# Order edges, four moved block differences and a rotation of three PSUM banks in a one-core decoder block

## The chip, the core and the metric

One core of a Trainium2 chip runs the whole program. The metric is device time in microseconds; of several executions the median is taken. The engines are TensorE (PE, with its weight loads as PEld), VectorE (DVE), ScalarE (ACT), GpSimd (POOL) and SyncE (SP), which issues the weight loads.

## The reference

A decoder block for 256 tokens of width 2048, in float32, one layer:

```python
h = h + hybrid_mixer(rmsnorm(h), ...)      # projection, GLA + short conv, gated merge, w_out
h = h + swiglu(rmsnorm(h), w_gate_up, w_down)
return rmsnorm(h, final_norm_w)

# hybrid_mixer
q, k, v, g_out, gk_low, gate_b, gate_c, xc, merge_a, merge_b = split(h @ w_in)
log_g = log_sigmoid(gk_low @ w_gk_up + b_gk_up) / 16
o = gla_chunked(q, k, v, log_g)            # 4 heads, chunks of 64: exp of cumulative decays
y_a = rmsnorm(o, gla_norm_w) * silu(g_out)
y_b = gate_b * causal_depthwise_conv(gate_c * xc, conv_w)     # 3 taps
merged = sigmoid(merge_a) * y_a + sigmoid(merge_b) * y_b
return merged @ w_out
```

The feed-forward width is 5632; the weights come to some 330 MB.

## The kernel before

**Products.** Every product is exact to nearly float32: each weight piece (128 x 1024 values, 512 KB) is loaded by SP, copied on ScalarE into a rounded high part (`high`, L217) and subtracted on VectorE to give a low part (`low`, L222); `mm3` (L326 to L328) does three matmuls for each product. A piece makes 12 full-width matmuls (128x512), or 24 of half that width. The code counts pieces in *ticks*; pieces are loaded five ticks ahead (`LOOK`), and `later`, `at` and `one_at_a_time` hang side work on ticks: a function runs, and so issues its instructions, at its tick.

**Stages.** First the GLA: for each of four heads `k`, `q` (columns) and `v` (tokens). Beside it the decay tables are built: `tables_within` (L673) makes `eq` and `ek` on VectorE and exponentiates `ek` (L678), L705 does `eq` at tick 23, `tables_across` (L682) makes `exk` and `exq` with five GpSimd instructions (L686 to L690) and exponentiates them (L691, L692). `decayed` (L722) multiplies a head's keys and queries by its part of the four tables (L726). `scores` (L730) multiplies them on PE into a score bank `sc_ps`, copies it out under a mask (L742) and without (L743), and splits it (L745, L747); `attend` (L754) is nine matmuls into two banks `o_ps` that alternate with the score banks. `x_blocks` (L711) prepares sums and differences of quarters of the normalized input, four blocks, at ticks 42, 47, 52 and 57: they are input to the next stage.

Then the gates: pairs of column groups (`gc` with `xc`, and so on) are done with seven block products in place of eight (`sevens`, 28 small pieces, five banks of `b0` to `b4`), and between these pieces stand the pieces of *plain groups* (`eights`, L354): `g`, `ma`, `gb`, `mb`. A plain group accumulates two banks (one for each half of the tokens) over eight pieces; then `gate`'s `done` empties them with a sigmoid or silu on ScalarE and a product on VectorE (`gated`, L840 to L844). `conv` (L806) shifts the pair's product by DMA and does five VectorE instructions (L827) at ticks 12 to 16 after; `merge` (L829) combines (L832, L833), and `transpose_block` (L541, bank `trb`) turns the merged half on PE.

Then `w_out` in four groups (`wo0` to `wo3`), each followed by `transpose_gain` (L524: two transpose groups `tr`, a scaled copy, high and low parts, and sums of blocks), then the feed-forward part in three rounds of `sevens` with plain groups, and down-projections `dn`, which take two of `b0` to `b5` in turn.

**PSUM.** Eight banks. `bank` without a tag deals `b0` to `b5` in turn (`k`, `q`, `v`, `wo`, `dn`); `aux` alternates `ax0` and `ax1` (scores, attention, `tr`); plain groups always take `b5` and `ax1`; `transpose_block` always takes `ax0`. A tile in a bank waits until the tile before it in that bank has been read.

**Order.** No order is written out for the engines. A planner goes through the instructions with its own durations; on each engine it issues, of those that it takes to be ready, the one that the code issued first. An instruction that it takes to be ready early can so pass others of its engine. On the chip every engine then works strictly in the planned order, and waits at each instruction for what it needs.

Of the kernel before, what the change touches and what calls it, by code (L numbers as in the profile page):

```python
# [8 lines left out]
F32 = mybir.dt.float32  # L9
F32R = mybir.dt.float32r  # L10
I8 = mybir.dt.int8
AF = mybir.ActivationFunctionType
ALU = mybir.AluOpType
AX = mybir.AxisListType

P = 128
T = 256
NT = T // P
# [147 lines left out]
@with_exitstack  # L166
def block_kernel(ctx, tc, x, xt, cols_in, gkw_in, gku_in, gnw, conv_w, finw, w_in, w_out, w_gu, w_dn, out):
    nc = tc.nc
    mats = {"w_in": w_in, "w_out": w_out, "w_gu": w_gu, "w_dn": w_dn}

    const = ctx.enter_context(tc.tile_pool(name="const", bufs=1))
# [8 lines left out]
    def bank(shape, name, tag=None):  # L180

        if tag is None:
            tag = f"b{turn['b'] % 6}"
            turn["b"] += 1
        return psum.tile(shape, F32, tag=tag, name=name)

    def aux(shape, name):

        turn["ax"] += 1
        return bank(shape, name, f"ax{turn['ax'] % 2}")  # L190

# [97 lines left out]
    def later(delay, fn):  # L292

        pending.append((count["tick"] + delay, fn))
# [35 lines left out]
    def tok_piece(ps, t, piece, k0, first, last, a):  # L330
        hi, lo, n = piece
        for k in range(n):
            ah, al = a(t, k0 + k)
            mm3(ps, ah, al, hi[:, k, :], lo[:, k, :], first and k == 0, last and k == n - 1)
# [16 lines left out]

        return lambda t, k: (hi[k // 4][:, k % 4, t * P:(t + 1) * P], lo[k // 4][:, k % 4, t * P:(t + 1) * P])

    def eights(key, a, done, tags=("b5", "ax1")):  # L354

        ps = [bank([P, 512], f"{key}_{t}", tag) for t, tag in enumerate(tags)]
        for k0 in range(0, KC, 2):
            piece, _ = yield
            for t in range(NT):
                tok_piece(ps[t], t, piece, k0, k0 == 0, k0 == KC - 2, a)  # L360
        done(ps)

    def quad(ps, pair, piece, first, last, onto=False):

# [119 lines left out]
    xh = aT.tile([P, KC, T], F32R, tag="ah", name="xh")  # L484
    xl = aT.tile([P, KC, T], F32R, tag="al", name="xl")
# [38 lines left out]
    def transpose_gain(q, hi, lo, tiles):  # L524

        raw = dpool.tile([P, 4, T], F32, tag="sg7", name="hraw")
        for m in range(2):
            ps = aux([P, 2, T], "tr")
            for j in range(2):
                for t in range(NT):  # L530
                    c = 4 * q + 2 * m + j
                    nc.tensor.transpose(out=ps[:, j, t * P:(t + 1) * P], in_=h[:, t, c * P:(c + 1) * P], identity=ident)
            for j in range(2):
                c = 4 * q + 2 * m + j
                nc.scalar.activation(raw[:, 2 * m + j, :], ps[:, j, :], AF.Copy, scale=ffc[:, c:c + 1])
        cs = slice(4 * q, 4 * q + 4)
        nc.scalar.copy(hi[:, cs, :], raw)
        nc.vector.tensor_tensor(out=lo[:, cs, :], in0=raw, in1=hi[:, cs, :].bitcast(F32), op=ALU.subtract)
        sum_blocks(raw, q, tiles, dpool.tile([P, 4, 2, P], F32, tag="sg8", name="hsum"))

    def transpose_block(src, t, hi, lo):  # L541

        ps = bank([P, 4, P], "trb", "ax0")
        for j in range(4):
            nc.tensor.transpose(out=ps[:, j, :], in_=src[:, j * P:(j + 1) * P], identity=ident)
        ts = slice(t * P, (t + 1) * P)
        nc.scalar.copy(hi[:, :, ts], ps)
        nc.vector.tensor_tensor(out=lo[:, :, ts], in0=ps, in1=hi[:, :, ts].bitcast(F32), op=ALU.subtract)
# [73 lines left out]
    for j in range(4):  # L622
        later(H_AT[j], lambda j=j: load_x(j))
        later(SQ_AT[j], lambda j=j: x_squares(j))
# [27 lines left out]
    eq = gpool.tile([P, NM, T], F32, tag="eq", name="eq")  # L652
    ek = gpool.tile([P, NM, T], F32, tag="ek", name="ek")

    inv = 1.0 / 16.0
# [12 lines left out]
    def sum_decay(m0):  # L668
        for m in range(m0, m0 + 4):
            nc.vector.tensor_tensor_scan(out=bc[:, m, :], data0=restart, data1=zm[:, m, :],  # L670
                                         initial=0.0, op0=ALU.mult, op1=ALU.add)

    def tables_within():  # L673

        for n in (0, 2):
            nc.vector.tensor_tensor(out=eq[:, :, n * C:(n + 1) * C], in0=ch(n), in1=last(n), op=ALU.subtract)
            nc.vector.tensor_copy(eq[:, :, (n + 1) * C:(n + 2) * C], ch(n + 1))
        nc.scalar.activation(ek, eq, AF.Exp, scale=-inv)  # L678

    across = {}  # L680

    def tables_across():  # L682

        exk = across["k"] = gpool.tile([P, NM, P], F32, tag="exk", name="exk")
        exq = across["q"] = gpool.tile([P, NM, P], F32, tag="exq", name="exq")
        nc.gpsimd.tensor_tensor(out=exk[:, :, 0:C], in0=last(0), in1=ch(0), op=ALU.subtract)  # L686
        nc.gpsimd.tensor_tensor(out=exk[:, :, 0:C], in0=exk[:, :, 0:C], in1=last(1), op=ALU.add)
        nc.gpsimd.tensor_tensor(out=exk[:, :, C:P], in0=last(1), in1=ch(1), op=ALU.subtract)
        nc.gpsimd.tensor_copy(exq[:, :, 0:C], ch(2))
        nc.gpsimd.tensor_tensor(out=exq[:, :, C:P], in0=ch(3), in1=last(2), op=ALU.add)  # L690
        nc.scalar.activation(exk, exk, AF.Exp, scale=inv)  # L691
        nc.scalar.activation(exq, exq, AF.Exp, scale=inv)  # L692

    def at(tick, fn):
        later(tick - count["tick"], fn)
# [6 lines left out]
    at(20, lambda: sum_decay(0))  # L702
    at(21, lambda: sum_decay(4))
    at(22, tables_within)
    at(23, lambda: nc.scalar.activation(eq, eq, AF.Exp, scale=inv))  # L705
    at(25, tables_across)


    xsums = (sT.tile([P, 4, 4, 2, P], F32R, tag="sh", name="sh"), sT.tile([P, 4, 4, 2, P], F32R, tag="sl", name="sl"))

    def x_blocks(q):  # L711
        pair = gpool.tile([P, NM, T], F32, tag="bc", name="xraw")
        raw, work = pair[:, 0:4, :], pair[:, 4:8, :].rearrange("p s (j c) -> p s j c", c=P)
        cs = slice(4 * q, 4 * q + 4)
        nc.vector.tensor_tensor(out=raw, in0=xh[:, cs, :].bitcast(F32), in1=xl[:, cs, :].bitcast(F32), op=ALU.add)
        sum_blocks(raw, q, xsums, work)

    for q in range(4):
        at(42 + 5 * q, lambda q=q: x_blocks(q))


    def decayed(i, kr, qr):  # L722
# [27 lines left out]
    o = [omain.tile([P, NT, DV], F32, tag=f"m{i}", name="o") for i in range(H)]  # L750
# [19 lines left out]
    for i in range(H):  # L770
# [20 lines left out]
        for t in range(NT):  # L791
            nc.scalar.activation(vh[:, t, :], vps[t], AF.Copy, scale=r1[:, t:t + 1])
            nc.vector.scalar_tensor_tensor(out=vl[:, t, :], in0=vps[t], scalar=r1[:, t:t + 1],
                                           in1=vh[:, t, :].bitcast(F32), op0=ALU.mult, op1=ALU.subtract)
# [9 lines left out]
    us, ya, sb, merge_at = {}, {}, {}, {}  # L804

    def conv(i):  # L806
        u = us[i]
        u1 = ew.tile([P, NT, 512], F32, tag="u1", name="u1")
        u2 = ew.tile([P, NT, 512], F32, tag="u2", name="u2")
        taps = ew.tile([P, 3, 512], F32, tag="taps", name="taps")  # L810
        nc.gpsimd.dma_start(taps, conv_w[:, :, i * 512:(i + 1) * 512].to_broadcast([P, 3, 512]))
        nc.gpsimd.memset(u1[0:1, 0, :], 0.0)
        nc.gpsimd.memset(u2[0:2, 0, :], 0.0)
        nc.gpsimd.dma_start(u1[1:113, :, :], u[0:112, :, :])
        nc.gpsimd.dma_start(u2[2:114, :, :], u[0:112, :, :])
        nc.gpsimd.dma_start(u1[113:128, :, :], u[112:127, :, :])
        nc.gpsimd.dma_start(u2[114:128, :, :], u[112:126, :, :])
        nc.gpsimd.dma_start(u1[0:1, 1, :], u[127:128, 0, :])
        nc.gpsimd.dma_start(u2[0:2, 1, :], u[126:128, 0, :])

        def taps_of(j):
            return taps[:, j:j + 1, :].to_broadcast([P, NT, 512])

        for n, (dst, src, by, op) in enumerate(((u1, u1, 1, ALU.mult), (u2, u2, 0, ALU.mult), (u, u, 2, ALU.mult),
                                                (u1, u1, u2, ALU.add), (u, u, u1, ALU.add))):
            by = taps_of(by) if isinstance(by, int) else by
            later(CONV_AT + n, lambda d=dst, s=src, y=by, o=op: nc.vector.tensor_tensor(out=d, in0=s, in1=y, op=o))  # L827

    def merge(i, ts):  # L829

        v = sb[i][:, ts, :]
        nc.vector.tensor_tensor(out=v, in0=v, in1=us[i][:, ts, :], op=ALU.mult)  # L832
        later(1, lambda: nc.vector.tensor_tensor(out=v, in0=v, in1=ya[i][:, ts, :], op=ALU.add))  # L833
        if mh[i] is None:
            mh[i] = omain.tile([P, 4, T], F32R, tag=f"m{i}", name="mh")
            ml[i] = oside.tile([P, 4, T], F32R, tag=f"m{i}", name="ml")
        for t in range(ts.start, ts.stop):
            one_at_a_time(3, lambda t=t: transpose_block(sb[i][:, t, :], t, mh[i], ml[i]))
# [29 lines left out]
    def gate_pair(pair):  # L868
# [8 lines left out]
        def done(t, one, two):  # L877
            if pair[0][:-1] == "gc":
                nc.vector.scalar_tensor_tensor(out=two, in0=one, scalar=r1sq[:, t:t + 1], in1=two,
                                               op0=ALU.mult, op1=ALU.mult)  # L880
                if t == 0:
                    later(1, lambda: conv(i))
                    merge_at[i] = count["tick"] + CONV_AT + 7
            else:
# [30 lines left out]
    for n in range(4):  # L915
        cs = slice(n * 512, (n + 1) * 512)
# [91 lines left out]
    for part, (f0, f1) in enumerate(PARTS):  # L1008
# [16 lines left out]
        for e in down:  # L1025
            key, k0 = e
            n = int(key.split("_")[1])
            c0, w = DOWN[part][n]
            cs = slice(c0, c0 + w)
# [24 lines left out]


CONV_AT = 12
H_AT = (2, 4, 6, 8)
SQ_AT = (5, 7, 9, 11)
WARM = 9
# [54 lines left out]
```

## Time and profile before

| | us |
|---|---|
| median of 3 runs (lowest, highest) | 1533.85 (1528.16, 1534.53) |
| the profiled execution, its own time | 1535.26 |
| its span, first to last instruction | 1533.6 |
| PE busy, share of the span | 1510.4, 98% |
| DVE busy | 1173.5, 77% |
| ACT busy | 832.1, 54% |
| POOL busy | 36.6, 2% |
| mean granted clock of TensorE | 0.996 |

Busy time of PE is that of pipelined matmuls: each overlaps the next, so the distance between two starts tells more than a duration. A note such as `[2.89 <-ACT sch L745]` behind an instruction says that its engine was idle for 2.89 us before it and what ended the idle time.

### The profile page before, as it was taken

The page shows a single profiled execution, that of the slowest core. Times are in us where ns is not written, and L with a number is a line of the kernel's source. Part 1 is how long each engine was busy: PE and PEld are TensorE (multiplying, and loading weights), DVE is VectorE, ACT ScalarE, POOL GpSimd, SP SyncE. Part 2 cuts the span into 40 slices and gives each one's busy share as a digit, 9 for nine tenths or more (in the row PEclk, how much of TensorE's full clock was granted, in tenths as well). Part 3 has the DMA queues.
Part 4 walks back from the last instruction along what each step waited for, and adds up shares of the span by engine and source line. Part 5 has one row for each costly group of instructions (what it writes and reads, how often), then busy time and mean ns, then how long its engine had stood idle before and what let it go on. Part 6 is the DMA issues. An engine that isn't in the chain of part 4 may idle for free.

```text
span 1533.6 us, 19370 instructions
## 1 busy us (share of the span) xinstructions
PE 1510.4 (98%) x7153; PEld 1262.0 (82%) x7153; DVE 1173.5 (77%) x1173; ACT 832.1 (54%) x936; POOL 36.6 (2%) x61
## 2 busy tenths in 40 slices
PE   9989999999999999999999999999999999999998
PEld 8979988888787788878788888888888888888887
DVE  5787557979879879965668899855889975678764
ACT  6755445555654555654556555633555653455543
POOL 0020000000000000000000000000000000000000
PEclk9999999999999999999999999999999999999999
DMA  9645557878776888786765767866677886566872
GB/s 321 222 150 158 172 158 248 276 228 259 260 246 212 286 261 257 242 263 206 224 178 178 263 221 250 312 200 178 219 248 224 273 272 192 178 229 197 249 222 92
DMA packets 96399, 346.00 MB, mean 226 GB/s; under 512 B 11092, under 2 KB 11220, under 8 KB 96176
## 3 DMA queue, kind: packets, MB, share of 16 engines
q1 hardware_dynamic: 92928, 333.77, 68.0%
q0 software_dynamic: 2944, 9.41, 2.5%
q10 hardware_dynamic: 432, 1.57, 0.3%
q8 instruction: 56, 0.92, 0.2%
q14 instruction: 39, 0.32, 0.1%
HBM read 338.45 MB, written 2.10 MB: 222 GB/s over the span
## 4 chain that ended last, share of the span: by engine, by line
PE 92%; DVE 3%; issue 1%; ACT 1%; DMA 1%; POOL 1%; SPq 0%; DVEq 0%; ACTq 0%
PE fg L326 7%; PE fg L328 7%; PE fg L327 7%; PE dn L326 5%; PE dn L327 5%; PE dn L328 5%; PE gc L326 3%; PE fu L326 3%; PE fu L328 3%; PE fu L327 3%; PE gc L328 3%; PE gc L327 3%; PE gb L326 2%; PE wo L326 2%; PE mb L326 2%; PE gb L327 2%
## 5 line engine op out<-in xcount | busy, mean ns | idle before, releaser
L222 DVE TENSOR_TENSOR lo<-raw,hi 128x1024 fp32r<-128x1024 f32 (+1 forms) x517 | 628.1, 1219 | 231.3 <-PE dn L326 74.8
L217 ACT CAST hi<-raw 128x1024 fp32r<-128x1024 f32 (+1 forms) x517 | 539.9, 1050 | 409.1 <-PE dn L328 114.1
L217 ACT CAST hi<-x 128x1024 fp32r<-128x1024 f32 x108 | 113.7, 1053 | 185.6 <-DVE x L244 130.0
L222 DVE TENSOR_TENSOR lo<-x,hi 128x1024 fp32r<-128x1024 f32 x108 | 132.1, 1223 | 31.8 <-ACT hi L217 18.7
L326 PE MATMUL dn<-lo,acth 128*128 128x512 f32 (+1 forms) x376 | 141.7, 377 | 0.0
L328 PE MATMUL dn<-hi,acth 128*128 128x512 f32 (+1 forms) x376 | 141.3, 376 | 0.0
L327 PE MATMUL dn<-hi,actl 128*128 128x512 f32 (+1 forms) x376 | 141.2, 376 | 0.0
L326 PE MATMUL fg<-lo,hh 128*128 128x512 f32 x312 | 121.6, 390 | 0.0
L328 PE MATMUL fg<-hi,hh 128*128 128x512 f32 x312 | 121.5, 389 | 0.0
L327 PE MATMUL fg<-hi,hl 128*128 128x512 f32 x312 | 121.4, 389 | 0.0
L244 DVE TENSOR_TENSOR x<-x,raw 128x1024 f32<-128x1024 f32 x72 | 87.9, 1220 | 7.2 <-DMA raw<-in_w_in_dram 3.5
L328 PEld LDWEIGHTS dn<-hi,acth 128*128 128x128 f32 x376 | 70.8, 188 | 13.0
L326 PEld LDWEIGHTS dn<-lo,acth 128*128 128x128 f32 x376 | 70.8, 188 | 12.7
L327 PEld LDWEIGHTS dn<-hi,actl 128*128 128x128 f32 x376 | 70.8, 188 | 12.6
L328 PE MATMUL fu<-hi,hh 128*128 128x512 f32 x192 | 74.7, 389 | 0.0
L326 PE MATMUL fu<-lo,hh 128*128 128x512 f32 x192 | 74.7, 389 | 0.0
L327 PE MATMUL fu<-hi,hl 128*128 128x512 f32 x192 | 74.7, 389 | 0.0
L326 PEld LDWEIGHTS fg<-lo,hh 128*128 128x128 f32 x312 | 58.6, 188 | 12.5 <-DVE h L1044 0.3
L328 PEld LDWEIGHTS fg<-hi,hh 128*128 128x128 f32 x312 | 58.6, 188 | 12.4
L327 PEld LDWEIGHTS fg<-hi,hl 128*128 128x128 f32 x312 | 58.6, 188 | 12.1
L326 PE MATMUL fg<-lo,sh 128*128 128x512 f32 x160 | 63.8, 399 | 0.0
L328 PE MATMUL fg<-hi,sh 128*128 128x512 f32 x160 | 62.5, 391 | 0.0
(245 smaller groups left out, 3067.8 us busy)
## 6 DMA issues: line engine op xcount, KB each, us to landing
raw<-in_w_in_dram SPq DMA_DIRECT2D x255, 512.0 KB, 4.6
raw<-in_w_gu_dram SPq DMA_DIRECT2D x176, 512.0 KB, 4.4
raw<-in_w_dn_dram SPq DMA_DIRECT2D x88, 512.0 KB, 4.3
raw<-in_w_out_dram SPq DMA_DIRECT2D x32, 512.0 KB, 4.2
x<-in_w_gu_dram SPq DMA_DIRECT2D x20, 512.0 KB, 5.4
y<-in_w_gu_dram SPq DMA_DIRECT2D x20, 512.0 KB, 3.9
y<-in_w_in_dram SPq DMA_DIRECT2D x16, 512.0 KB, 4.2
x<-in_w_in_dram SPq DMA_DIRECT2D x16, 512.0 KB, 4.9
```

Of the source, the lines that this page charges most:

```text
L217: nc.scalar.copy(hi[:, ks, :], raw[:, ks, :])
L222: nc.vector.tensor_tensor(out=lo[:, ks, :], in0=raw[:, ks, :], in1=hi[:, ks, :].bitcast(F32), op=ALU.subtract)
L244: nc.vector.tensor_tensor(out=x, in0=x, in1=other, op=ALU.add)
L326: nc.tensor.matmul(ps, lhsT=sh, rhs=ml, start=first, stop=False, skip_group_check=onto)
L327: nc.tensor.matmul(ps, lhsT=sl, rhs=mh, start=False, stop=False, skip_group_check=onto)
L328: nc.tensor.matmul(ps, lhsT=sh, rhs=mh, start=False, stop=last, skip_group_check=onto)
```

## The change

Five edits. (1) A planner edge puts the exponentials of `exk` and `exq` behind that of `eq` on ScalarE (`issue_after`: order of issue, no wait for its end). (2) The first instruction of each of the four `x_blocks` is kept behind whatever VectorE instruction the code issued just before it (`pin`), and the blocks go to ticks 50, 54, 58 and 62. (3) The convolution's five and (4) the merge's two VectorE instructions are kept in the same way. (5) Plain groups take two of three banks, `b5`, `ax0` and `ax1`, in turn; both kinds of transposes take, each time, the oldest one that no open group holds. `g0` keeps `b3` and `b4`.

```diff
+    pin = tc.keep_in_program_order
...
+    lent = ["b5", "ax0", "ax1"]
...
-    def eights(key, a, done, tags=("b5", "ax1")):
-
-        ps = [bank([P, 512], f"{key}_{t}", tag) for t, tag in enumerate(tags)]
+    def eights(key, a, done, tags=None):
+
+        mine = tags or [lent.pop(0) for _ in range(NT)]
+        ps = [bank([P, 512], f"{key}_{t}", tag) for t, tag in enumerate(mine)]
...
         done(ps)
+        if tags is None:
+            lent.extend(mine)
...
-            ps = aux([P, 2, T], "tr")
+            lent.append(lent.pop(0))
+            ps = bank([P, 2, T], "tr", lent[-1])
...
-        ps = bank([P, 4, P], "trb", "ax0")
+        lent.append(lent.pop(0))
+        ps = bank([P, 4, P], "trb", lent[-1])
...
+    first_exp = []
...
-        nc.scalar.activation(ek, eq, AF.Exp, scale=-inv)
+        first_exp.append(nc.scalar.activation(ek, eq, AF.Exp, scale=-inv).ins)
...
-        nc.scalar.activation(exk, exk, AF.Exp, scale=inv)
-        nc.scalar.activation(exq, exq, AF.Exp, scale=inv)
+        with tc.issue_after(first_exp[-1]):
+            nc.scalar.activation(exk, exk, AF.Exp, scale=inv)
+            nc.scalar.activation(exq, exq, AF.Exp, scale=inv)
...
-    at(23, lambda: nc.scalar.activation(eq, eq, AF.Exp, scale=inv))
+    at(23, lambda: first_exp.append(nc.scalar.activation(eq, eq, AF.Exp, scale=inv).ins))
...
-        nc.vector.tensor_tensor(out=raw, in0=xh[:, cs, :].bitcast(F32), in1=xl[:, cs, :].bitcast(F32), op=ALU.add)
+        pin(nc.vector.tensor_tensor(out=raw, in0=xh[:, cs, :].bitcast(F32), in1=xl[:, cs, :].bitcast(F32), op=ALU.add))
...
-        at(42 + 5 * q, lambda q=q: x_blocks(q))
+        at(X_AT[q], lambda q=q: x_blocks(q))
...
-            later(CONV_AT + n, lambda d=dst, s=src, y=by, o=op: nc.vector.tensor_tensor(out=d, in0=s, in1=y, op=o))
+            later(CONV_AT + n, lambda d=dst, s=src, y=by, o=op: pin(nc.vector.tensor_tensor(out=d, in0=s, in1=y, op=o)))
...
-        nc.vector.tensor_tensor(out=v, in0=v, in1=us[i][:, ts, :], op=ALU.mult)
-        later(1, lambda: nc.vector.tensor_tensor(out=v, in0=v, in1=ya[i][:, ts, :], op=ALU.add))
+        pin(nc.vector.tensor_tensor(out=v, in0=v, in1=us[i][:, ts, :], op=ALU.mult))
+        later(1, lambda: pin(nc.vector.tensor_tensor(out=v, in0=v, in1=ya[i][:, ts, :], op=ALU.add)))
...
+X_AT = (50, 54, 58, 62)
```

## Rows read from the trace of the kernel before

**Rows 1.** The page, first part: busy us, share of the span, instructions.

```profile
PE 1510.4 (98%) x7153; PEld 1262.0 (82%) x7153; DVE 1173.5 (77%) x1173; ACT 832.1 (54%) x936; POOL 36.6 (2%) x61
```

**Rows 2.** Stretches: length, busy us (instructions) by engine, granted clock, DMA share, GB/s.

```profile
100.00:120.00 20.00, 15.08 (x69) 11.99 (x69) 19.24 (x31) 13.27 (x21) 0.62 (x2) 0.83 0.49 149
120.00:240.00 120.00, 120.00 (x712) 107.18 (x711) 69.40 (x81) 52.87 (x69) 2.19 (x4) 1.00 0.59 177
480.00:540.00 60.00, 56.53 (x248) 45.06 (x247) 52.46 (x50) 32.91 (x37) 0.52 (x1) 1.00 0.75 258
800.00:820.00 20.00, 20.00 (x94) 16.66 (x93) 14.25 (x16) 12.26 (x18) 0.00 (x0) 1.00 0.53 159
820.00:840.00 20.00, 20.00 (x94) 16.36 (x93) 19.92 (x24) 15.29 (x22) 0.00 (x0) 1.00 0.62 179
```

**Rows 3.** Timeline of TensorE, scores and attention: start, length, instruction [idle before, releaser].

```profile
95.53 1.05 PE L737 MATMUL sc_ps<-eq,ek 128*128 128x128 f32 x8
...
101.40 0.39 PE L328 MATMUL v<-hi,xh 128*128 128x512 f32 x1
...
103.44 0.39 PE L328 MATMUL v<-hi,xh 128*128 128x512 f32 x1
106.72 0.49 PE L326 MATMUL o_ps<-vl,sch 128*128 128x512 f32 x1 [2.89 <-ACT sch L745]
...
109.98 0.80 PE L326 MATMUL o_ps<-vl,sch 128*128 128x512 f32 x1 [1.78 <-ACT scr L743]
...
115.95 0.40 PE L328 MATMUL v<-hi,xh 128*128 128x512 f32 x1
```

**Rows 4.** Timeline of ScalarE, exponentials of the tables.

```profile
85.65 1.06 ACT L691 ACTIVATE exk<-exk 128x1024 f32<-128x1024 f32 x1 [7.20 <-POOL exk L687]
...
88.20 1.90 ACT L678 ACTIVATE ek<-eq 128x2048 f32<-128x2048 f32 x1
```

**Rows 5.** Timeline of GpSimd, the tables across chunks.

```profile
77.53 6.08 POOL L686 TENSOR_TENSOR exk<-bc 128x512 f32<-128x512 f32 x1 [26.90 <-DVE bc L670]
...
86.15 1.05 POOL L690 TENSOR_TENSOR exq<-bc 128x512 f32<-128x512 f32 x1
```

**Rows 6.** Timeline of VectorE, tables to scores.

```profile
80.01 0.42 DVE L677 COPY eq<-bc 128x512 f32<-128x512 f32 x1
...
82.62 0.75 DVE L777 TENSOR_TENSOR kr<-k,rb 128x256 f32<-128x256 f32 x2
90.13 0.69 DVE L726 TENSOR_TENSOR ek<-ek,kr 128x512 f32<-128x512 f32 x1 [6.76 <-ACT ek L678]
...
94.96 0.42 DVE L726 TENSOR_TENSOR exk<-exk,kr 128x256 f32<-128x256 f32 x1
...
98.31 1.22 DVE L715 TENSOR_TENSOR xraw<-xh,xl 128x1024 f32<-128x1024 f32 x1
...
105.40 0.43 DVE L742 COPY_PREDICATED scr<-mask,sc_ps 128x256 f32<-128x256 int8 x1
```

**Rows 7.** Waits of TensorE, 235 to 760: us in total, times, longest.

```profile
PE gb L326 <- DVE ya L844: 3.0, 3, 1.5
PE g L326 <- DVE sb L844: 1.4, 1, 1.4
...
PE ma L326 <- ACT ya L853: 1.0, 1, 1.0
...
PE gc L326 <- DVE lo L222: 0.5, 2, 0.3
```

**Rows 8.** Timeline of TensorE, from the last `ma` group to `gb`.

```profile
683.88 0.39 PE L328 MATMUL ma<-hi,xh 128*128 128x512 f32 x1
685.78 0.50 PE L326 MATMUL gb<-lo,xh 128*128 128x512 f32 x1 [1.52 <-DVE ya L844]
```

**Rows 9.** Timeline of VectorE, the second merge's sum.

```profile
492.32 1.22 DVE L833 TENSOR_TENSOR sb<-sb,ya 128x1024 f32<-128x1024 f32 x1
```

**Rows 10.** Waits of VectorE, 340 to 760: us in total, times, longest.

```profile
DVE u L827 <- DMA u<-u: 7.8, 2, 4.4
```

## Prediction

> **What bounds the kernel now.** I read the page's first part, then the stretch table, then TensorE's own timeline and its waits. PE is busy for 1510.4 of 1533.6 us [rows 1], so only its 23 us of idle time, and any time at the low clock, can be won. Some 10 us of that lie at the very start and end, which the change does not touch. Of the rest the largest piece is one stretch: between 100 and 120 us PE is busy for 15.08 of 20 us and its granted clock averages 0.83; from 120 to 240 us it never pauses [rows 2]. The other losses are single waits between 240 and 760 us [rows 7].
>
> The timeline of the bad stretch [rows 3] is to be read by distances between starts. A full-width matmul normally starts 0.227 us after the one before it (9 steps from 101.40 to 103.44). From the `v` matmul at 103.44 to the one at 115.95 there are 18 such steps, which should take 4.09 us and took 12.51: **8.42 us lost**. Two waits make most of it: 2.89 us for the head's split scores, 1.78 us for the copy of the next head's. The 14 steps from 109.98 to 115.95 then average 0.43 us, the 1.2 GHz level; the granted clock fell after these two pauses.
>
> Why are the scores late? ScalarE had nothing to do for 7.20 us because `exk`'s exponential was at the head of its queue and GpSimd had not finished that table; `ek`'s exponential, whose input VectorE had completed by 80.43, ran behind it at 88.20 [rows 4 to 6]. VectorE in turn waited 6.76 us for `ek` [rows 6]. Then, from 98.31, `x_blocks` took VectorE: the masked copy of scores that were computed at 95.53 to 96.8 [rows 3] ran only at 105.40 [rows 6]. I counted the order of VectorE's instructions against the order in which the code issues them: the first of the four `x_blocks` runs 35 places early, the fourth 45. Nothing needs their result before the first gate group with products of sums, at about 240 us.
>
> **The change part by part.**
>
> *Exponentials.* With `exk` and `exq` queued behind `eq`, ScalarE can run `ek` at about 80.5 (1.90 us), one weight cast (the size of `exk`, 1.06) and `eq` (the size of `ek`), to about 85.4; `exk`'s input is there at 85.6 and `exq`'s at 87.2 [rows 4, 5]. The last of the first head's four products, at 94.96 before [rows 6], could then come near 89. PE reaches its score matmuls at 95.53 in any case, so this alone removes little; it frees VectorE and ScalarE of the pile of casts and low parts that they worked off between 90 and 106.
>
> *x_blocks.* One block is two instructions of 1.22 us and four of 0.42 on VectorE (lengths of [rows 6]) with a cast on ScalarE: 4.1 us. Two blocks lay between the scores and the attention. At ticks 50 to 62 they fall into some 35 us that end just before the gates; VectorE is busy for 69.40 of 120 us between 120 and 240 [rows 2], and 4 x 4.1 = 16.4 us fit. Cover gone, a block delays PE by at most its 4.1 us, but PE does not pause once in that stretch with VectorE 58% busy, so I take 0. With both edits the masked copy follows its scores at about 97.5, the rest of that chain took 1.32 us before (105.40 to PE's start at 106.72), so it ends near 99 to 100, and PE asks at 103.67. The second head's scores come one piece of twelve matmuls and the score matmuls behind, some 4 us, and their bank must be copied out before the fourth attention matmul, at 104.35. That makes it with about 2 us to spare. Bounds: 0 to 8.42 us gained; I take all of **8.4**, since both releasers of PE's two waits sit behind the moved work, and without the pauses the clock has no cause to fall.
>
> *Three banks for plain groups.* A plain group had `b5` and `ax1`, always; the next group's first matmul waited for the sigmoid and the product on the last one. Following `lent` by hand through the gate list, the next group's first bank is a free one each time, and its second bank is the one that the last group filled first, asked for six matmuls (1.36 us) later. The recorded waits are 3.0 us (three times, `gb`), 1.4 (`g`) and 1.0 (`ma`) [rows 7]. A wait costs more than its record: at 683.88 PE's next start came 1.90 us later instead of 0.227 [rows 8], and 0.11 more at the step after, 1.78 lost for 1.52 recorded, so 0.26 on top. The first two `gb` and `ma` go: 1.5 + 1.0 + 3 x 0.26 = 3.3 us. The last `gb` keeps something: its second bank is emptied when PE restarted before, 685.78, and is now asked for at 683.88 + 0.23 + 1.36 = 685.47, so about 0.4 of 1.78 stays: 1.4. For `g` (1.4 + 0.26) I take 0: VectorE is busy for 52.46 of 60 us there, and two matmul pieces later PE's transposes wait for a merge sum that ends at 493.54 [rows 9]; if PE comes earlier it waits longer there. Its bounds are 0 and 1.7. Sum: **4.7**.
>
> *Transposes.* They rotate over the three banks when no group is open. One meets trouble. Following both counters, the third output group `wo2` takes `b4` and `b5`, and right after its first piece the second transpose group of block 1 (`tr`) is handed `b5`. It must wait for the whole of `wo2`, some 20 us. PE's queue can pass it, because the planner sees the bank taken; what moves is block 1's conversion, again 4.1 us of VectorE, from `wo2` into `wo3`, after about 800. There VectorE is busy for 14.25 of 20 us, then 19.92 of 20 [rows 2]. 5.75 us of room take 4.1, and PE needs block 1 only behind the whole of `wo3`, 8 pieces of 2.72 us later. I take 0. Bounds: 0, and 4.1 plus one wait as long as `g`'s 1.4 [rows 7], 5.5 lost.
>
> *Convolution and merge kept in order.* In the counted order the convolution's products run only 4 to 9 places early, the merges within 3. VectorE waited for the convolution's transfers twice, 7.8 us [rows 10], and PE did not notice. Kept behind the preceding instruction, they stall VectorE less, and the merges stay where they are. Behind a late merge stand the next low parts and PE's transposes. Bounds: 0.5 gained (what PE loses from 480 to 540 [rows 2] beyond the `g` and `ma` waits, 3.47 - 1.7 - 1.3) and one 1.22 us instruction per merge lost, 4.9; I take 0, the value that the unchanged merge order suggests.
>
> **Sum.** 8.4 + 4.7 = 13.1 us. The profiled execution took 1535.26 us (span 1533.6), 1.4 over the median of 1533.85. So 1522.2 against its own time, **1521** against the median.
>
> **A rule that speaks against it.** GpSimd's first table subtraction took 6.08 us while VectorE ran without a break to 83.37, and the last of the same size, with VectorE idle, 1.05 [rows 5, 6]. The Trainium skill (SBUF — State Buffer, "Who interferes with whom") says that a VectorE instruction with two SBUF inputs and a GpSimd instruction that reads SBUF exclude each other, each holding the port for one whole instruction. By that rule each of the four later table instructions would wait for one VectorE instruction at most: 4 x (1.22 + 1.05) = 9.1 us after 83.6, the tables at 92.7, still before 95.53, and the sum stands. The row is worse than the rule: all of VectorE's instructions in those 6 us went ahead. That makes the rival below.
>
> **Rivals.**
>
> 1. *GpSimd starved* (slower). Before, VectorE stood idle for 6.76 us and that is when GpSimd finished. With `ek` early VectorE is busy. If each of the four remaining table instructions takes 6.08 us [rows 5], `exq`'s input comes at 83.6 + 24.3 = 107.9, its products at about 110, and PE, whose queue holds the score matmuls at 95.53, waits 14.5 us; with the second head and the low clock some 19 in place of 8.4. Net 10.6 lost, 4.7 gained: 1540. It costs from the point where `exq` is ready after 92.5, and eats the whole gain at about 105. Against it: VectorE's queue itself stops at the first product with an `ex` table, after some 5 us of work, and then GpSimd runs free. Chance 0.08.
> 2. *Only half of the attention's wait goes*: the second head's scores are still late, 4 of the 8.4 us stay, and part of the bank gain too: 1525 to 1529. For it: that bank's margin is only 2 us. Chance 0.15.
> 3. *VectorE takes back the bank gain*: every early PE start ends in a wait for a low part, as in the stretch from 480 to 540, where PE loses 3.47 of 60 us [rows 2]: 8.4 alone, 1525.5. Against it: PE's recorded waits for a low part are 0.5 us in two places in all of the gates [rows 7]. Chance 0.14.
> 4. *The planner undoes it*: new order elsewhere, or `tr`'s bank wait at its 5.5 us upper bound with a late attention; no net change, 1530 to 1535. Chance 0.08.
>
> **How the numbers follow.** The forecast has 0.55, with its own range 1515 to 1525. If every pause between 100 and 760 us went (8.4 and the 12 of the single waits), the time would be 1513. The range 1512 to 1532 leaves out rival 1 and part of rival 4. What a measurement of this kernel can tell from no change is about 0.5%, 7.7 us: faster means below 1526.2, slower above 1541.5. Faster: the forecast, and about half of rivals 2 and 3: 0.71. Slower: half of rival 1 and a case that I don't see, 0.09. The rest, 0.20, is the same.
>
> **What would show it.** Right: `ek`'s exponential at 80 to 81 and before `exk`'s; masked copies within 2 us of the score matmuls; no `o_ps` wait over 0.5 us, and a granted clock of 1.00 from 100 to 120; `x_blocks` after 160 us; no wait of `gb` or `ma` for `ya`, while PE's waits for merge sums and low parts near 490 to 520 grow by what the `g` wait gives up; `tr` of block 1 after 800. Wrong: `exq`'s table after 95, scores waiting on it, or any PE wait over 2 us that was not there.

## The result and the profile after

The changed kernel takes 1517.73 us (median of 4 runs, 1516.4 to 1518.36) against 1533.3 for the kernel before on the same chip: a ratio of 0.9904 [0.988, 0.9927], **15.6 us faster**. The forecast was 1521. The profiled execution took 1517.46 us (span 1515.8), 17.8 less than the profiled one of before.

The first line of the page after, beside [rows 1]:

```profile
PE 1502.8 (99%) x7153; PEld 1259.4 (83%) x7153; DVE 1177.3 (78%) x1173; ACT 832.3 (55%) x936; POOL 33.7 (2%) x61
```

TensorE's busy time fell by 7.6 us with as many matmuls as before, for two reasons. At the low clock each matmul lasted longer: of the 8.5 us lost in the attention before, the two pauses are 4.7, and most of the remaining 3.8 were counted as busy. And a wait is recorded shorter than the delay that it makes [rows 8]. So the 17.8 us are counted by distances between starts. For each matmul of either trace I took the distance to the next start, less the usual distance for its width (0.227 us for 512 columns, 0.120 for 256, 0.109 for a transpose), and summed the excess by place:

| excess of TensorE, us | before | after |
|---|---|---|
| start of the program, to 20 us | 3.19 | 3.07 |
| attention, 100 to 120 us | 8.48 | 0.03 |
| `gb`, three times | 3.85 | 0 |
| `ma` | 1.32 | 0 |
| `g` (before for its bank, after for a low part) | 1.68 | 0.47 |
| transposes for a merge (`trb`) | 0.73 | 0.24 |
| `gc`, first one | 1.08 | 0.62 |
| `gc` for a low part | 1.40 | 0.76 |
| `tr` for `h` | 1.84 | 1.16 |
| all else | 1.35 | 0.76 |
| sum | 24.92 | 7.11 |

For the nine matmuls of the warm-up the usual distance is 0.427 us. The rows are those of two executions, which lie 2.2 us further apart than the medians.

The stretches after, in the columns of [rows 2] (length, busy us and instructions of PE, PEld, DVE, ACT, POOL, granted clock, DMA share, GB/s):

```profile
100.00:120.00 20.00, 20.00 (x132) 18.33 (x131) 12.74 (x17) 14.96 (x26) 0.62 (x2) 1.00 0.57 180
120.00:240.00 120.00, 119.66 (x682) 105.38 (x682) 82.48 (x100) 56.03 (x69) 2.18 (x4) 1.00 0.59 181
480.00:540.00 60.00, 59.81 (x267) 49.35 (x268) 51.18 (x49) 36.61 (x39) 0.00 (x0) 1.00 0.82 272
```

From 100 to 120 us TensorE now runs 132 matmuls in place of 69, at a granted clock of 1.00 in place of 0.83. VectorE has 6.5 us less to do there and 13 us more in the next stretch, where `x_blocks` now runs, at 160 to 204 us. Its timeline shows the first (start, length, instruction):

```profile
160.45 1.22 DVE L726 TENSOR_TENSOR xraw<-xh,xl 128x1024 f32<-128x1024 f32 x1
161.70 1.55 DVE L444 TENSOR_TENSOR xraw<-xraw 128x256 f32<-128x256 f32 x4
```

TensorE's timeline answers to [rows 3]: the attention starts 0.22 us behind the last `v` matmul, where 3.28 us lay between them.

```profile
95.16 1.05 PE L748 MATMUL sc_ps<-eq,ek 128*128 128x128 f32 x8
...
103.08 0.39 PE L331 MATMUL v<-hi,xh 128*128 128x512 f32 x1
103.30 0.39 PE L329 MATMUL o_ps<-vl,sch 128*128 128x512 f32 x1
103.53 0.39 PE L330 MATMUL o_ps<-vh,scl 128*128 128x512 f32 x1
```

ScalarE, beside [rows 4]: `ek` first, then `exk`, which no longer finds an unfinished table (no note of idle time).

```profile
83.35 1.28 ACT L688 ACT_TABLE_LOAD   x1 [6.34 <-DVE eq L687]
84.65 1.93 ACT L688 ACTIVATE ek<-eq 128x2048 f32<-128x2048 f32 x1
...
90.16 1.05 ACT L702 ACTIVATE exk<-exk 128x1024 f32<-128x1024 f32 x1
91.12 1.05 ACT L703 ACTIVATE exq<-exq 128x1024 f32<-128x1024 f32 x1
```

VectorE, beside the masked copy at 105.40 in [rows 6]: both heads' copies have been made before TensorE asks.

```profile
98.96 0.44 DVE L753 COPY_PREDICATED scr<-mask,sc_ps 128x256 f32<-128x256 int8 x1
...
101.89 0.44 DVE L753 COPY_PREDICATED scr<-mask,sc_ps 128x256 f32<-128x256 int8 x1
```

TensorE's waits of 235 to 760 us, where [rows 7] had waits of 3.0, 1.4 and 1.0 us (us in total, times, longest): no `gb` and no `ma` is left.

```profile
PE tr L539 <- DVE h L936: 0.9, 1, 0.9
PE gc L329 <- DVE lo L225: 0.5, 1, 0.5
PE g L329 <- DVE lo L225: 0.2, 1, 0.2
```

### The profile page after: what moved, and what is told of

It reads as the page before. It is cut to its first block, busy times and chain, and to the rows that moved or that the text cites. A ratio compares the mean times of both kernels' runs of the same rounds, so it can differ in the third digit from the quotient of the medians.

```text
span 1515.8 us, 19369 instructions
## 1 busy us (share of the span) xinstructions
PE 1502.8 (99%) x7153; PEld 1259.4 (83%) x7153; DVE 1177.3 (78%) x1173; ACT 832.3 (55%) x936; POOL 33.7 (2%) x61
## 4 chain that ended last, share of the span: by engine, by line
PE 95%; DVE 2%; DMA 1%; issue 1%; ACT 1%; SPq 0%; DVEq 0%; ACTq 0%
PE fg L329 7%; PE fg L331 7%; PE fg L330 7%; PE dn L329 5%; PE dn L330 5%; PE dn L331 5%; PE gc L329 3%; PE gc L330 3%; PE gc L331 3%; PE fu L329 3%; PE fu L331 3%; PE fu L330 3%; PE v L330 2%; PE wo L329 2%; PE v L329 2%; PE gb L329 2%
```

## The experiments

Every kernel was timed beside the kernel before on one chip, in four groups: the changed kernel, e1 to e4, e5 to e8, e9 to e12. Times of one group compare best; the median of the kernel before moved by 1.6 us between groups.

| kernel | us | before, same group | ratio, 95% interval |
|---|---|---|---|
| changed kernel | 1517.73 | 1533.3 | 0.9904 [0.988, 0.9927] |
| e1: exponentials alone | 1527.86 | 1533.41 | 0.9966 [0.9953, 0.9979] |
| e2: `x_blocks` alone | 1526.83 | 1533.41 | 0.9959 [0.9946, 0.9971] |
| e3: banks alone | 1528.47 | 1533.41 | 0.9970 [0.9958, 0.9981] |
| e4: convolution and merge alone | 1530.83 | 1533.41 | 0.9989 [0.9980, 0.9998] |
| e5: exponentials and `x_blocks` | 1525.56 | 1533.51 | 0.9943 [0.9931, 0.9956] |
| e6: changed, no pin on convolution and merge | 1519.89 | 1533.51 | 0.9915 [0.9901, 0.9928] |
| e7: changed, no pin on the merge | 1517.96 | 1533.51 | 0.9899 [0.9885, 0.9912] |
| e8: changed, no pin on the convolution | 1520.00 | 1533.51 | 0.9913 [0.9899, 0.9927] |
| e9: before, tables on VectorE | 1525.69 | 1531.91 | 0.9964 [0.9953, 0.9975] |
| e10: before, `x_blocks` pinned at the old ticks | 1526.08 | 1531.91 | 0.9968 [0.9958, 0.9978] |
| e11: changed, GpSimd's tables late | 1525.01 | 1531.91 | 0.9965 [0.9953, 0.9978] |
| e12: changed, tables on VectorE | 1518.78 | 1531.91 | 0.9921 [0.9907, 0.9934] |

### e1, the exponentials alone

```diff
-        nc.scalar.activation(ek, eq, AF.Exp, scale=-inv)
+        first_exp.append(nc.scalar.activation(ek, eq, AF.Exp, scale=-inv).ins)
...
+        with tc.issue_after(first_exp[-1]):
+            nc.scalar.activation(exk, exk, AF.Exp, scale=inv)
+            nc.scalar.activation(exq, exq, AF.Exp, scale=inv)
```

> The kernel before with the order edge of the exponentials alone. Theory A (the block differences hold the masked copies back; the exponentials alone remove little): the attention's two waits stay, at least 6 of the 8.4 us, time 1531 to 1533, ratio to before 0.998 to 1.001. Rival B (ScalarE waiting for GpSimd is the cause): the waits of o_ps fall under 1 us and the time to about 1525, ratio 0.995.

5.5 us faster: theory A falls, and rival B's waits of under 1 us did not come either. VectorE's timeline shows that the first of the `x_blocks` still goes ahead of the masked copy, as before; but both run 5.01 us earlier (93.30 for 98.31, 100.39 for 105.40):

```profile
93.30 1.21 DVE L718 TENSOR_TENSOR xraw<-xh,xl 128x1024 f32<-128x1024 f32 x1
...
100.39 0.43 DVE L745 COPY_PREDICATED scr<-mask,sc_ps 128x256 f32<-128x256 int8 x1
```

TensorE's waits and the stretch from 100 to 120 us:

```profile
PE o_ps L326 <- DVE vl L796: 1.3, 1, 1.3
PE g L326 <- DVE sb L847: 1.3, 1, 1.3
PE o_ps L326 <- ACT scr L746: 1.2, 1, 1.2
```

```profile
100.00:120.00 20.00, 17.50 (x106) 15.08 (x105) 19.71 (x31) 16.31 (x29) 0.62 (x2) 1.00 0.46 151
```

Two pauses stand in the stretch: 1.2 us for the copy of the scores, where 2.89 and 1.78 had stood [rows 3], and 1.3 us at 114.95, ten us later, for a low part of `v`. The granted clock is 1.00 behind them. So part of the gain is the pauses and part the clock.

### e2, `x_blocks` alone, and e10, its pin without the new ticks

```diff
-        nc.vector.tensor_tensor(out=raw, in0=xh[:, cs, :].bitcast(F32), ...)
+        pin(nc.vector.tensor_tensor(out=raw, in0=xh[:, cs, :].bitcast(F32), ...))
...
-        at(42 + 5 * q, lambda q=q: x_blocks(q))
+        at(X_AT[q], lambda q=q: x_blocks(q))          # e2 only
```

> The kernel before with the four block differences alone kept in order and put at ticks 50 to 62. Theory A: the masked copies follow their score matmuls within 3 us, no o_ps wait over 0.5 us, granted clock 1.00 from 100 to 120; 7.5 to 8.5 us gained, 1525, ratio 0.9945. Rival B (without the early exponentials the second head's scores stay late): half stays, 1529, ratio 0.997.

> The kernel before with x_blocks' first sum kept in program order at its old ticks, 42 to 57; with the new ticks as well it took 1526.8 us. In the plan the four sums stand some ten VectorE instructions earlier than there, all behind the masked copies of the first two heads. The ticks without the pin give the same plan as the kernel before, instruction by instruction. Theory A (the pin does it, the ticks add nothing): 1526 to 1527.5, the o_ps wait about 1 us. Rival B (the earlier tick brings the sums into VectorE's way again): 1528 or more, with a wait of o_ps or of v above 1.5 us.

e2 gained 6.6 us by the medians, e10 5.8, with overlapping intervals: the pin is what acts, as theory A of e10 has it. Neither theory of e2 came out: 6.6 lies between the 7.5 to 8.5 of the one and the half of the other. In both one wait of 1.0 us is left, since `ek` is as late as before (88.27 in e2) and the masked copies come at 101.78 and 104.71 (e2). This is the wait of the fourth attention matmul for the second head's score bank, whose margin the prediction had worked out. TensorE's wait in e2:

```profile
PE o_ps L327 <- ACT scr L744: 1.0, 1, 1.0
```

### e3, the three banks alone

```diff
-    def eights(key, a, done, tags=("b5", "ax1")):
+    def eights(key, a, done, tags=None):
+        mine = tags or [lent.pop(0) for _ in range(NT)]
...
-        ps = bank([P, 4, P], "trb", "ax0")
+        lent.append(lent.pop(0))
+        ps = bank([P, 4, P], "trb", lent[-1])
```

> The kernel before with the three banks in turn alone. Theory C (forecast): the gb and ma waits go but VectorE takes back what the g wait gives, 4.7 us gained, 1528.6, ratio 0.997; PE's waits for merge sums and low parts from 480 to 525 grow by 1 to 2 us. Rival D (the banks alone also free the g wait, as seen after): 6.5 to 7 us gained, 1526.5, and no new waits there.

4.9 us faster (2.9 to 6.4 by the interval), as the prediction's term of 4.7. The waits for `ya` and for `g`'s bank are gone, and most of what `g` gave up, 1.4 us, came back in front of the merge, as the prediction had it: the wait there grew from 0.5 to 1.8 us. TensorE's waits, the merge's before, then all of e3 from 235 to 760 us.

```profile
PE trb L545 <- DVE sb L833: 0.5, 1, 0.5
```

```profile
PE trb L551 <- DVE sb L839: 1.8, 1, 1.8
PE tr L537 <- DVE h L931: 1.4, 1, 1.4
PE gc L327 <- DVE lo L223: 0.6, 2, 0.3
```

### e4, convolution and merge alone

```diff
-            later(CONV_AT + n, lambda ...: nc.vector.tensor_tensor(out=d, in0=s, in1=y, op=o))
+            later(CONV_AT + n, lambda ...: pin(nc.vector.tensor_tensor(out=d, in0=s, in1=y, op=o)))
...
-        nc.vector.tensor_tensor(out=v, in0=v, in1=us[i][:, ts, :], op=ALU.mult)
-        later(1, lambda: nc.vector.tensor_tensor(out=v, in0=v, in1=ya[i][:, ts, :], op=ALU.add))
+        pin(nc.vector.tensor_tensor(out=v, in0=v, in1=us[i][:, ts, :], op=ALU.mult))
+        later(1, lambda: pin(nc.vector.tensor_tensor(out=v, in0=v, in1=ya[i][:, ts, :], op=ALU.add)))
```

> The kernel before with convolution and merge alone kept in order. Theory E (from the trace after: the convolution's products no longer go ahead of the sums of weight pieces on which the next casts wait, which frees VectorE before 410 and from 460 to 520): the waits of PE for low parts and for the merge sum, 0.3 + 0.9 + 0.6 us, go, and about 0.5 us more of the g wait; 2 to 2.5 us gained, 1531, ratio 0.9985. Rival F (forecast: no effect): 1533, the low parts' waits as before.

2.6 us faster by the medians, [0.3, 3.1] by the interval: a small gain, not the 0 of the prediction. The low-part waits at 515 and 519 us, `ma`'s wait and the first of `g`'s for its bank are gone. New are two low-part waits (0.5 us at 390, 0.7 before `g` at 488) and one of 1.7 us before a later `g`, for its bank, which neither e3 nor the changed kernel has.

### e5, both edits of the attention

e1's and e2's edits together.

> The kernel before with the exponentials' edge and with x_blocks kept in order at ticks 50 to 62; two banks, convolution and merge as before. Alone the first gave 5.5 us and the second 6.6. Theory A (both act on the same 8.4 us that TensorE loses from 103 to 116 us, so they overlap): 8 to 9 us below the kernel before, 1524.5 to 1525.5; no o_ps wait of TensorE is left, the stretch from 100 to 120 us is busy for 19.9 of 20. Rival B (the gains add): 12 us, 1521.5, which would need a loss elsewhere to go too. Rival C (the gates' waits grow when TensorE comes earlier): under 7 us, over 1526. GpSimd: its first table subtraction took 6.08 us in the kernel before and with each edit alone, 1.93 us with all edits; if the order of instructions decides it, this kernel has 1.93, if it is a chance of the start, either.

8.0 us faster, theory A. Alone they gave 5.5 and 6.6: they act on the same 8.48 us. The stretch is full:

```profile
100.00:120.00 20.00, 20.00 (x131) 18.33 (x131) 11.43 (x16) 14.22 (x25) 0.31 (x1) 1.00 0.47 147
```

The waits of the gates are as before (`gb` 2.7 us in 3, `g` 1.6, `ma` 1.0). GpSimd's first table took 6.08 us here as well, so the order of the instructions does not decide that.

### e6, e7 and e8: the changed kernel without both pins, without the merge's, without the convolution's

The removals are those lines of e4's diff.

> The changed kernel without the pins on the convolution's products and on the merge; all else as changed. This is the sum that the prediction made, which took the pins at 0. Theory A (the pins are worth what they gave alone, 2.6 us, and more by what the three banks give up at a merge sum): 2.5 to 3.5 us slower than the changed kernel, 1520 to 1521.5, with TensorE's transposes waiting for a merge sum near 470 to 490 us for about 1.9 us as with the three banks alone, and a wait for low parts near 500 us. Rival B (the pins' gain alone came from bank waits that three banks remove anyway): the same as the changed kernel within 0.7 us.

> The changed kernel with the convolution's products pinned and the merge not. The plan then differs from the changed kernel's by two moved VectorE instructions and nine TensorE rows. Theory A (the merge sum that the transposes wait for is what matters, and it is early because the convolution's products ahead of it stall no longer): the same as the changed kernel within 0.7 us. Rival B (the pin on the merge itself brings it early): 1.5 to 2.5 us slower, with the wait of the transposes for the merge sum of about 1.9 us back.

> The changed kernel with the merge pinned and the convolution's products not. Theory A: 2 to 3 us slower than the changed kernel (the convolution's pin is what the pins gain), VectorE again waiting some us for the convolution's transfers, and low parts or the merge sum behind them late for TensorE near 490 to 520 us. Rival B (the merge's pin is it): the same within 0.7 us. Rival C: faster by up to 0.7 us, since the convolution's products in the changed kernel, behind the low parts' sums at 352 to 364 us, are followed by a wait of TensorE for a low part at 382 us (0.6 us) that the kernel before does not have.

Measured side by side: without the merge's pin 1517.96 (1517.35 to 1518.53), the changed kernel's time; without the convolution's 1520.00 (1518.7 to 1522.9); without both 1519.89 (1518.77 to 1522.93). So the convolution's pin is worth about 2 us on top of the other edits, and the merge's nothing that can be seen. TensorE's waits at the second merge and near it, first in e6, then in e8; in the changed kernel and in e7 it does not wait at this merge, but for a low part just before it (0.2 and 1.1 us; e7 has a wait of 0.5 at a later merge):

```profile
PE trb L552 <- DVE sb L843: 1.8, 1, 1.8
PE gc L328 <- DVE lo L224: 0.6, 2, 0.4
```

```profile
PE trb L552 <- DVE sb L843: 1.8, 1, 1.8
```

Counted as in the excess table, in the 16 us from the last matmul of the second `mb` group on, TensorE loses 2.4 us in e6 and 3.2 in e8, 0.7 in the changed kernel and 1.6 in e7.

Why a pin on the convolution helps a later merge is read from ScalarE's queue. The merge needs the product with `mb`, and that needs `mb`'s two sigmoids. ScalarE in e6, not pinned:

```profile
472.65 1.06 ACT L219 CAST hi<-x 128x1024 fp32r<-128x1024 f32 x1 [4.23 <-DVE x L246]
473.61 1.05 ACT L219 CAST hi<-raw 128x1024 fp32r<-128x1024 f32 x1
474.56 1.23 ACT L853 ACTIVATE mb<-mb,r 128x512 f32<-128x512 f32 x2
```

The changed kernel:

```profile
471.87 0.66 ACT L854 ACTIVATE mb<-mb,r 128x512 f32<-128x512 f32 x1 [1.10 <-PE mb L331]
473.23 0.66 ACT L854 ACTIVATE mb<-mb,r 128x512 f32<-128x512 f32 x1 [0.70 <-PE mb L331]
474.42 1.05 ACT L220 CAST hi<-x 128x1024 fp32r<-128x1024 f32 x1 [0.53 <-DVE x L247]
```

TensorE started its last `mb` matmul at 472.34 in e6 and at 472.80 in the changed kernel. Pinned, each sigmoid waits for TensorE alone. Unpinned, both stand behind two casts, and for the first of these ScalarE waited 4.23 us, until VectorE had made a sum of weight pieces. All fourteen profiles show this group so: without the convolution's pin (nine) the first sigmoid starts 2.0 to 3.0 us behind the start of that matmul, with it (five) 0.9 us before.

VectorE: the convolution's last product, the product with `mb` and the merge sum, in e6 and then in the changed kernel:

```profile
469.05 1.22 DVE L837 TENSOR_TENSOR u<-u,u 128x1024 f32<-128x1024 f32 x1
...
476.02 1.28 DVE L854 TENSOR_TENSOR sb<-sb,mb 128x512 f32<-128x512 f32 x2
...
480.75 1.22 DVE L843 TENSOR_TENSOR sb<-sb,ya 128x1024 f32<-128x1024 f32 x1
```

```profile
469.71 1.22 DVE L838 TENSOR_TENSOR u<-u,u 128x1024 f32<-128x1024 f32 x1
...
474.25 1.27 DVE L855 TENSOR_TENSOR sb<-sb,mb 128x512 f32<-128x512 f32 x2
...
480.05 1.22 DVE L844 TENSOR_TENSOR sb<-sb,ya 128x1024 f32<-128x1024 f32 x1
```

The convolution itself is not late without its pin: in e6 its last product runs 0.7 us earlier. Late is the product with `mb`, by 1.8 us, right behind its sigmoids; the merge sum ends 0.7 us later, and 1.2 later counted from TensorE's last `mb` matmul. That the sigmoids' place makes the whole 2 us is read from the traces, not tested by an edit of its own.

### e9 and e12: the tables on VectorE

```diff
-        nc.gpsimd.tensor_tensor(out=exk[:, :, 0:C], in0=last(0), in1=ch(0), op=ALU.subtract)
+        nc.vector.tensor_tensor(out=exk[:, :, 0:C], in0=last(0), in1=ch(0), op=ALU.subtract)
...                                       # and so the four others; e9 on before, e12 on the changed kernel
```

> The kernel before with the five table instructions of exk and exq on VectorE in place of GpSimd; no edge, no pin, no bank is changed. It tests by another way whether the queue of ScalarE, standing behind a table that GpSimd has not finished, was the first cause. On VectorE the five cost three of 0.68 and two of 0.42 to 0.68 us, some 3 us of its time, and ScalarE gets ek's input before exk's. Theory A (the queue was the cause): the 7.2 us of ScalarE and the 6.8 us of VectorE's wait for ek go, and the gain is that of the exponentials' edge alone, 5.5 us, less at most the 3 us: 1528 to 1531. Rival B (GpSimd's slowness was not what mattered, only x_blocks): within 0.7 us of the kernel before, o_ps waits of 2.7 and 1.5 us unchanged.

> The changed kernel with the five table instructions on VectorE, so that no GpSimd work runs beside VectorE there. Theory A (in the changed kernel GpSimd's tables are hidden, whichever engine goes first): within 0.7 us of the changed kernel, 1517 to 1518.4. Rival B (the tables still cost TensorE something): faster by over 0.7 us. Rival C (3 us more on VectorE before the scores): slower by 0.7 to 3 us, with a wait of TensorE for sc_ps or o_ps.

e9 gained as much as the edge (0.9964 against 0.9966), without any edge: `ek` is exponentiated at 81.49, before `exk` (87.94), and VectorE's wait for it is gone. This agrees with ScalarE's queue behind GpSimd's table as the first cause. It does not show the queue alone, since the plan also places `x_blocks` differently there (first sum at 95.96), and the time came out below the 1528 to 1531 of theory A. e12 is 1 us above the changed kernel's time, by the ratios to the kernel before 2.6, and the intervals overlap; within 0.7 was theory A's. It is not faster, and TensorE waits neither for scores nor in the attention: that GpSimd makes the tables costs nothing that can be seen in the changed kernel. e12's profile has a wait of 1.2 us at a later merge, which the changed kernel's has not; whether the tables have to do with it is open.

### e11, the first rival made to happen

```diff
-        nc.gpsimd.tensor_tensor(out=exk[:, :, 0:C], in0=last(0), in1=ch(0), op=ALU.subtract)
+        for _ in range(9):
+            nc.gpsimd.tensor_tensor(out=exk[:, :, 0:C], in0=last(0), in1=ch(0), op=ALU.subtract)
```

> The changed kernel with GpSimd's first table subtraction done nine times over (the same result each time), so that exk's and exq's inputs come 8.4 us later at 1.05 us each and up to 14 us later where VectorE runs beside it. It makes the prediction's first rival happen. In the changed kernel exq's exponential began at 91.1 us behind other work, its input having been there since 84.2 (in other profiles 89.0). Theory A (late tables delay TensorE's scores one for one once the slack is used): exq's exponential begins at 95 to 103, TensorE's score matmuls wait, and the run is 2 to 10 us slower than the changed kernel, 1520 to 1528, with the low clock if TensorE stands still for over 2 us. Rival B (the work behind is reordered by the engines' own slack): within 0.7 us of the changed kernel.

Theory A: 7.3 us above the changed kernel's time, and 6.2 above e12's, timed beside it. `exq`'s exponential began at 99.67, 8.55 us later than after the change. The late table was `exk`'s, which ended at 98.67; `exq`'s had ended at 90.95, and its exponential stood behind that of `exk` on ScalarE. TensorE's timeline, and its stretch:

```profile
95.30 0.94 PE L749 MATMUL sc_ps<-eq,ek 128*128 128x128 f32 x7
101.31 1.19 PE L751 MATMUL sc_ps<-exq,exk 128*128 128x128 f32 x4 [5.07 <-DVE exq L738]
102.16 0.77 PE L329 MATMUL v<-lo,xh 128*128 128x512 f32 x1
```

```profile
100.00:120.00 20.00, 18.69 (x90) 16.18 (x91) 15.34 (x23) 15.86 (x24) 0.62 (x2) 0.83 0.57 174
```

The pause cost 5.2 us. The ten steps from 102.16 to 106.57 then averaged 0.44 us in place of 0.227, the 1.2 GHz level: 2.1 more.

## Why the prediction was right, and where it was not

**The attention, 8.4 us: right.** 8.45 went by the excess table, 8.0 by e5. The steps that it named are in the trace: masked copies 2.3 and 1.2 us behind their scores (within 2 was forecast), no `o_ps` wait, the second head's bank copied out 1.3 us before it was asked for (about 2 were forecast), clock 1.00, `x_blocks` from 160 us without one wait of TensorE for them. The price of nothing for their new place stands.

**"This alone removes little": wrong.** The exponentials alone gave 5.5 us. The step looked at one use of the tables, the score matmuls at 95.53, which indeed did not move, and stopped. It had itself written that the edit frees VectorE of a pile of work between 90 and 106, and did not follow that pile to its end: everything behind it in VectorE's order, the `x_blocks` with the masked copy behind them, moved by 5.01 us (e1). The sum was not hurt, since both edits were priced together.

**`ek` at 80 to 81: right in order, not in time.** It ran at 84.65 in the profile after, at 81.0 to 81.7 with the same edge in e1, e11 and e12. The 3 us between the two are GpSimd's race with VectorE (last section). What is left is the load of the table of functions ahead of it, 1.28 us on ScalarE (at 83.35 in the profile after), which the prediction did not have. There was slack for both.

**The three banks, 4.7 us: right.** e3 gave 4.9. In the excess table the `gb` and `ma` waits gave 5.2 against the 4.7 of the prediction; the 0.4 us that the last `gb` was to keep did not show. That `g` gains next to nothing by itself is e3 too: of its 1.4 us, 1.3 turned up at the merge.

**`tr` in the third bank, 0: right.** Block 1's two `tr` groups stood side by side before; now the second runs 21.6 us behind the first, at 783.35 directly ahead of block 2's, and TensorE starts it without a wait:

```profile
783.12 0.39 PE L331 MATMUL wo<-hi,mh 128*128 128x512 f32 x1
783.35 0.60 PE L539 MATMUL tr<-ident,h 128*128 128x128 f32 x4
```

**Convolution and merge, 0: this is the step that failed**, by about 2 us of the 2.5 between the sum's 13.1 and the 15.6 measured. Its sentence was that the products "stall VectorE less, and the merges stay where they are". I had counted places in VectorE's order alone. What the traces show moved by the pin is ScalarE's order: unpinned, the sigmoids of the second `mb` group stand behind a cast for which ScalarE waits 4.23 us (e6); pinned, they run at once, the merge sum ends 1.2 us earlier behind TensorE's last `mb` matmul, and the wait of 1.8 us at the merge goes. That is the wait for which the prediction gave `g` nothing: in both terms the merge sum was treated as fixed. Without the pins the sum as made is what the chip gives: e6 took 1519.89, 13.6 us less than before, where 13.1 had been worked out.

The remaining 0.5 us are less than the medians move from group to group.

**The rivals.** GpSimd starved: it did not come. e11, where more GpSimd work and not starvation made a table late, shows that a late table is paid for as the rival had it, with the low clock on top. The point was set too early: `exq`'s exponential began at 99.67 in e11 and TensorE waited 5.07, so a table that is ready by 94.6 costs nothing; the prediction had 92.5. Its premise was too hard: only the first table instruction takes 6.08 us; behind it, with VectorE at work, they took 1.0 to 1.6 (e5). Half of the attention stays: not with both edits; of the 8.5 us 3.2 stay in e1's trace and 1.6 in e2's. VectorE takes back the bank gain: e3 has it in part, 1.3 us more at the merge, and the convolution's pin removes it; what is new in the changed kernel is one low part at 382 us, 0.76 us of excess, and one before `g` at 480, 0.47. The planner undoes it: no.

Not separated: which half of the bank edit, the plain groups or the transposes, gives the 4.9. No version measured beats the changed kernel by more than can be told; e7 equals it with one pin less.

## What to carry to other kernels

When an edit takes a stall from an engine that is not the bound, follow its whole queue to the next place where the bound asks, not only the result that was stalled. And when an edit changes the order on one engine, look at the order on the others too: twice here an instruction that was ready stood on ScalarE behind one whose input another engine had not finished, first `ek`'s exponential behind `exk`'s (7.20 us), then `mb`'s sigmoids behind a cast (4.23 us), and the second time an edit on VectorE moved it. Where two edits work on one wait, price them together; here 5.5 and 6.6 make 8.0.

## What the runs showed of the hardware

**GpSimd beside VectorE.** Eleven of the twelve profiles with the tables on GpSimd show the first table instruction at 6.07 or 6.08 us, with VectorE's at their usual 0.68 and 0.42 ([rows 5, 6]). The profile after alone shows the two sharing; GpSimd, then VectorE:

```profile
77.40 1.93 POOL L696 TENSOR_TENSOR exk<-bc 128x512 f32<-128x512 f32 x1 [26.88 <-DVE bc L678]
79.30 1.48 POOL L698 TENSOR_TENSOR exk<-bc 128x512 f32<-128x512 f32 x1
```

```profile
78.35 1.52 DVE L686 TENSOR_TENSOR eq<-bc 128x512 f32<-128x512 f32 x1
79.80 1.26 DVE L687 COPY eq<-bc 128x512 f32<-128x512 f32 x1
```

GpSimd started 0.17 us behind the same VectorE instruction in both cases, so the start does not tell them apart. In each of the eleven it ended 0.90 us behind the end of the last `low` in VectorE's run (before: 83.60 and 82.70); in the profile after it ended 0.90 us behind the end of the first (79.33 and 78.42). So these traces read as if it was held up and then took the same time; what decides after which VectorE instruction it comes in is open. The rule that the prediction weighed (the Trainium skill, SBUF — State Buffer, "Who interferes with whom": each engine holds the port for one whole instruction) fits the shared case and the later tables, not the 6.08 us, in which six more VectorE instructions went ahead.

**The clock.** Pauses of 1.2 and 1.3 us within 10 us left the granted clock at 1.00 (e1), as did a single one of 1.8 (e8). The pair of 2.89 and 1.78 [rows 3] and the single one of 5.07 (e11) were followed by steps at the low level, for 14 and 10 matmuls.
